# A hybrid decoder layer on one core: the order of the work up to the end of attention, read from a table

## The chip, the core and the metric

The kernel runs on one core of a Trainium2 chip. A core has five engines that run side by side: TensorE (PE, matrix products into PSUM), VectorE (DVE), ScalarE (ACT), GpSimd (POOL) and SyncE (SP), which here issues the transfers between memory and SBUF. Each engine has an instruction stream of its own and carries it out in order; streams meet at semaphores. The metric is the device time of one execution in microseconds, the median of several runs.

## What is computed

One layer (DEPTH is 1) over 1024 tokens of width 1024, in float32:

```python
h = rms_norm(x, norm1_g[layer])
proj = h @ w_in[layer]
q, k, v, glu_a, glu_b = jnp.split(proj, splits, axis=-1)      # 512 columns each
q = rms_norm(q.reshape(bsz, seq, ATTN_HEADS, HEAD_DIM), q_norm_g[layer])
k = rms_norm(k.reshape(bsz, seq, ATTN_HEADS, HEAD_DIM), k_norm_g[layer])
attn = stick_breaking_attention(q, k, v).reshape(bsz, seq, ATTN_WIDTH)
c = glu_a * jax.nn.sigmoid(glu_b)
c = causal_depthwise_conv(c, conv_dw_w[layer], conv_dw_b[layer])      # 31 taps
c = jax.nn.silu(layer_norm(c, conv_ln_g[layer], conv_ln_b[layer]))
x = x + jnp.concatenate([attn, c], axis=-1) @ w_out[layer]
h = rms_norm(x, norm2_g[layer])
gate, val = jnp.split(h @ w_up[layer], 2, axis=-1)
gate = jax.nn.silu(causal_depthwise_conv(gate, ffn_dw_w[layer], ffn_dw_b[layer]))
x = x + (gate * val) @ w_down[layer]
```

Attention has 8 heads of 64 columns, no softmax: the weight of key s for query t is sigmoid(z[t, s]) times the product of (1 - sigmoid(z[t, j])) over the keys j between s and t.

## The kernel before

**Numbers.** A float32 product is made of operands that are each split into a high part and a rest (`hi`, `lo`). Three matmuls (lines 325 to 327, function `mm3`) stand for one product. So each weight and each activation needs a cast (ACT: the high part) and a subtraction (DVE or POOL: the rest).

**Stages.** First part, in one plan of 1874 operations: the norm of x and its transposes (lines 422 to 449), the weights of the projections (loaded at 475, cast at 479, split at 483), the projections of v, of the two halves of the GLU, of q and k (601, 659, 935, 989), the convolution (taps on DVE at 696 to 708, terms on ACT at 722 and POOL at 725, end at 737 to 740, its layer norm at 761 to 820), attention, and the half of the output projection that belongs to the convolution (1345). Second part, in a plan of 237 operations: the half of the output projection that belongs to attention (`opa`), the second norm, and the operands for a Strassen-like form of the up projection. Then the feed-forward part (`up`, and the down projection at 1848) in an order written out by hand.

**Attention.** For each head and each half of the queries: the doubled queries come by a transfer (1124), are transposed (1129), copied with their gain (ACT, 1133) and reduced to the rest (DVE, 1136). For each block of 128 queries the scores `z` are two matmuls (1172, 1173) into one of two PSUM banks; ACT makes 1 - sigmoid of them (1180); DVE runs the product along the keys as a scan (1194); POOL or ACT subtracts one (1199, 1201). Two query blocks go together: per pair of key blocks PE transposes the weights (`wT`, 1221), the high part is copied by ACT or DVE (1230, 1232), the rest made by DVE (1237, 1242), and PE multiplies them with v (`po`, 1249). At the end of a half ACT and DVE copy `po` out (1277, 1280).

**Order.** `Plan.add` (line 94) takes an operation: the engines that it may run on with a cost in ns for each, a function that emits it, a key (about when it is due), the operations that it comes after, and the buffers that it takes (`token`). An operation's number is its place among the calls of `add`. `Plan.run` (line 124) then picks operation after operation: of those that are ready and due (`HORIZON`) it takes the one that can start first by the costs (`PATIENCE` lets an earlier key go first), sends it to the engine where it would end first, hands it its buffers, and calls the function. The order in which functions are called is the order of each engine's stream (`in_order` adds dependences that hold it). The model of `run` adds 60 ns for a hand-over between engines, 130 to POOL, 170 behind PE; it makes POOL and a shared DVE operation (`"DVE2"`) wait for each other; a transfer costs a latency and 2.6 ns per KB.

Of the kernel before, what the change touches and what calls it, by code (L numbers as in the profile page):

```python
# [11 lines left out]
AF = mybir.ActivationFunctionType  # L12
# [28 lines left out]
HORIZON, PATIENCE = 3.0, 150  # L41
# [19 lines left out]


class Plan:


    HAND_OVER, POOL_HAND_OVER = 60, 130
# [5 lines left out]
    class Op:  # L72
        __slots__ = ("cost", "emit", "key", "after", "takes", "end", "engine", "n", "kb", "dmas", "shares")

    def __init__(self, slots, in_turn):
# [20 lines left out]
    def add(self, cost, *args):  # L96
        if not isinstance(cost, dict):
            cost, args = {cost: args[0]}, (lambda eng, f=args[1]: f(),) + args[2:]
        op = Plan.Op()
        op.shares = "DVE2" in cost  # L100
        op.cost, op.emit, op.key = {e.rstrip("2"): c for e, c in cost.items()}, args[0], args[1]
        op.after = list(args[2]) if len(args) > 2 else []
        op.takes = list(args[3]) if len(args) > 3 else []
        op.end, op.engine, op.n, op.kb, op.dmas = None, None, len(self.ops), 512, 1
        self.ops.append(op)
        return op
# [17 lines left out]
    def run(self, busy):  # L124
        at = {e: busy.get(e, 0.0) for e in ("PE", "ACT", "DVE", "POOL", "SP")}
        over = {"PE": 0, "ACT": 100, "DVE": 80, "POOL": 40, "SP": 0}
# [4 lines left out]
        open_ = {op.n: len(set(o.n for o in op.after)) for op in self.ops}  # L131
        nexts = {}
        for op in self.ops:
            for n in set(o.n for o in op.after):
                nexts.setdefault(n, []).append(op)
        ready = [op for op in self.ops if open_[op.n] == 0]
        left = {id(t): len(set(o.n for o in t.users)) for t in self.tokens}
        done, dma, landed, holds = 0, 0.0, [], {"DVE": 0.0, "POOL": 0.0}
        main = sorted(self.ops, key=lambda op: op.key)
        low = 0  # L140
        while done < len(self.ops):
            while main[low].end is not None:
                low += 1
            horizon = main[low].key + HORIZON
            best = None
            for op in ready:
                if op.key > horizon:
                    continue
                slots = self.slots_for(op.takes)
                if slots is None:  # L150
                    continue
                room = max([at_ for at_, _ in slots], default=0.0)
                mine = None
                for e, cost in op.cost.items():
                    r = room
                    for o in op.after:
                        r = max(r, o.end + (0 if o.engine == e else Plan.POOL_HAND_OVER if e == "POOL" else Plan.HAND_OVER)
                                + (170 if o.engine == "PE" and e != "PE" else 0))
                    start = max(r, at[e])
                    if e == "SP":  # L160
                        start = max(start, landed[-8]) if len(landed) > 7 else start
                    if e == "POOL" or e == "DVE" and op.shares:
                        cost += min(cost, max(0, holds["DVE" if e == "POOL" else "POOL"] - start))
                    if mine is None or start + cost < mine[0]:
                        mine = (start + cost, e, cost, start)
                _, e, cost, start = mine
                rank = (max(start - PATIENCE, at[e]), op.key) if op.key <= main[low].key + 1 else (start, op.key)
                if best is None or rank < best[0]:
                    best = (rank, op, e, cost, start)
            assert best is not None, "the plan is stuck"  # L170
            _, op, e, cost, start = best
            for t, slot in zip(op.takes, self.slots_for(op.takes)):
# [5 lines left out]
            if e == "POOL" or e == "DVE" and op.shares:  # L178

                other = "DVE" if e == "POOL" else "POOL"  # L180
                at[other] += min(op.cost[e], max(0, holds[other] - start))
                holds[e] = op.end
            if e == "SP":

                at[e] = start
                for _ in range(op.dmas):
                    at[e] = max(at[e] + 60, landed[-8] if len(landed) > 7 else 0)
                    dma = max(dma, at[e] + (2300 if start < 3000 else 1300)) + op.kb * 2.6 / op.dmas
                    landed.append(dma + 600)
                op.end = landed[-1]  # L190
            else:
                at[e] = op.end - over[e]
            op.emit(e)
            ready.remove(op)
            done += 1
# [4 lines left out]
            for o in nexts.get(op.n, []):  # L200
                open_[o.n] -= 1
                if open_[o.n] == 0:
                    ready.append(o)
# [4 lines left out]
def kernel(  # L208
# [169 lines left out]
    for n in range(2):  # L378
# [12 lines left out]
                in_turn=("nb", "wt", "th", "tl", "thd", "tld", "kst", "vst", "q", "qd"))  # L391
    add = plan.add

    def T(us):

        return (us - FIRST_STAGE) / 8.0
# [28 lines left out]
    def norm_in(t, x, at_):  # L425
# [9 lines left out]
        c = add("DVE", 1290, lambda: nc.vector.scalar_tensor_tensor(xt, xt, d["rs"], g1, op0=ALU.mult, op1=ALU.mult), T(at_), [b])  # L435
# [29 lines left out]
    def weights(name, srcs, shape, at_, key=None, homes=None):  # L465
# [15 lines left out]
        x = add("SP", 3500, load, T(at_ - LEAD_LOAD) if key is None else key, [], [room])  # L481
        a = add("ACT", 1060, high, T(at_ - LEAD_W), [x], d["rooms"])
        b = add({"DVE": 1300, "POOL": 2450}, lambda eng: (nc.vector if eng == "DVE" else nc.gpsimd).tensor_tensor(
# [10 lines left out]
    def differences(blk, key, after, tokens):  # L494
# [17 lines left out]
        x.kb, x.dmas = 1024, 6  # L512
        subs = []
        for n in range(2):
# [4 lines left out]
            subs.append(add({"POOL": 2560}, sub, key, [x]))  # L519
# [13 lines left out]
    def normalized(name, d, o, m, to, at_):  # L533
# [17 lines left out]
        a = add("ACT", 3500, square, T(at_), [c], [r])  # L551
        b = add("POOL", 2700, lambda: rstd(d["rs"], d["sq"], 1.0 / DH), T(at_), [a])
        a = add("ACT", 1850, scale, T(at_), [b])
# [3 lines left out]
    def summed(name, d, o, m, to, at_):  # L557
# [22 lines left out]
        a = add("ACT", 620, square, key, [m], [room, r])  # L580
        b = add("DVE", 690, lambda: nc.vector.tensor_reduce(d["sq"], groups(d["squares"]), axis=AX.X, op=ALU.add), key, [a])
        c = add("POOL", 1900, lambda: rstd(d["rs"], d["sq"], 1.0 / DH), key, [b])
        e = add({"ACT": 1850, "DVE2": 1900}, scale, key, [c])
# [5 lines left out]
    def project(name, parts, ws, t, at_, room):  # L589
# [3 lines left out]
        for k in range(ND):  # L593
# [7 lines left out]
            m = add("PE", 685, products, T(at_ + 0.7 * k), [ws[k // 2]["ready"], h_ready[t][k // 4]] + ([m] if m else [] if name == "v" else list(norm_done)), [] if m else [o])  # L601
# [36 lines left out]
    def glu(c, ws, ats, conv_at, conv_to):  # L638
# [8 lines left out]
        for n, at_ in zip(range(2), ats):  # L647
            gate = None
            for j, part in enumerate("ba"):
                o, m = plan.token("o"), None  # L650
                e = {}
                for k in range(ND):
# [6 lines left out]
                    m = add("PE", 685, products, T(at_ + 5.5 * j + 0.68 * k), [ws[part]["ready"]] + [h_ready[t][k // 4] for t in range(4 * n, 4 * n + 4)] + ([m] if m else []),  # L659
# [27 lines left out]
        last = add({"POOL": 1360, "DVE": 700}, both_sums, key(0, 1), bodies + norm_done + params_ready, [xsum, cacc])  # L687
# [24 lines left out]
        for m in range(HALF + 1):  # L712
            coef = (lambda m=m: tap_sum(c, HALF - 1 - m)) if m < HALF else (lambda: tap(c, 0))
            if m == 0:
                last = add("ACT", 720, lambda coef=coef: nc.scalar.activation(
# [9 lines left out]
            last = add("POOL", 1310, lambda e=e: nc.gpsimd.tensor_tensor(d["c"], d["c"], e["t"], op=ALU.add), key(m, 16), [x, last])  # L725
# [11 lines left out]
        first = add("ACT", 820, shifted, key(1, 1), [b] + co_free, [co_tokens[c]] if c < 3 else [])  # L737
        e1 = add("DVE", 760, lambda: nc.vector.tensor_tensor(d["c"], d["c"], d["a"], op=ALU.subtract), key(1, 1), [last, a, b])
        e2 = add("DVE", 760, lambda: nc.vector.tensor_tensor(out_view()[:, 0, :], d["a"], out_view()[:, 0, :], op=ALU.add), key(1, 1), [first, b, e1])
        e3 = add("DVE", 760, lambda: nc.vector.tensor_tensor(out_view()[:, 1, :], d["c"], d["b"], op=ALU.subtract), key(1, 1), [e1, e2])  # L740
# [11 lines left out]
    def conv_norm(n, at_):  # L752
        half = slice(n * HS, (n + 1) * HS)
        d, normed = {}, []
        for t in range(4):
# [18 lines left out]
            b = add("DVE", 800, stats, k, [a], [r])  # L774
            c = add("POOL", 1450, lambda t=t: rstd(d["rs", t], d["mv", t][:, 1:2], 1.0), k, [b])
            f = add("DVE", 690, normal, k, [c] + conv_normed)
# [4 lines left out]
        for c in range(4):  # L781
# [31 lines left out]
            b = add("ACT", 620, gate, k, [a], [r])  # L813
            f = add("ACT", 620, lambda c=c, dst=dst: nc.scalar.activation(dst(), d["pt", c], AF.Identity, scale=par("lg", c), bias=par("lb", c)), k, [b])
            m = add("POOL", 1310, lambda c=c, dst=dst: nc.gpsimd.tensor_tensor(dst(), dst(), d["gate", c], op=ALU.mult), k, [f])
# [3 lines left out]
            h = add("ACT", 560, high, k, [m] + stores, two if c % 2 == 0 else [])  # L819
            e = add({"DVE": 690, "POOL": 1310}, lambda eng, parts=parts, dst=dst: (nc.vector if eng == "DVE" else nc.gpsimd).tensor_tensor(  # L820
# [7 lines left out]
            if c % 2:  # L828
# [4 lines left out]
                x = add("SP", 4000, store, k, [e])  # L833
                conv_stored[n].append(x)
# [7 lines left out]
    def params():  # L842
# [15 lines left out]
        x.kb = 60  # L858
# [1030 lines left out]
```

## Time and profile before

| | us |
|---|---|
| median of 3 runs | 1120.7 (1119.34 to 1120.95) |
| span of the profiled execution, first to last instruction | 1118.1 |
| PE busy in the span | 1094.5 (98%) |
| DVE busy | 884.7 (79%) |
| ACT busy | 618.6 (55%) |
| POOL busy | 546.6 (49%) |

The span is one execution, taken by the hardware profiler; the runs are timed apart from it. In the lines of the profile, `L1172` is line 1172 of the kernel, `z<-keys` says what an instruction writes and reads, PEld is the loading of a matmul's stationary operand, and an arrow at the end names the instruction that ended the wait in front. The first part of the kernel ends near 430 us, the second near 500 us, and the rest is the feed-forward part.

### The profile page before, as it was taken

What the parts mean: (1) busy time and instruction counts of PE and PEld (TensorE: products, weight loads), DVE (VectorE), ACT (ScalarE), POOL (GpSimd) and SP (SyncE); (2) the same over time, 40 slices, a digit from 0 to 9 for tenths busy, and PEclk for the clock granted to TensorE, in tenths of its full rate; (3) what the DMA queues carried; (4) which work ended last, traced back from release to release, by engine and by line L of the source; (5) the groups of instructions that cost most, each with busy time, mean ns of one, the idle gap of its engine ahead of it and who ended that gap; (6) DMA issues with size and microseconds to landing.
All of it is one profiled execution on the core that took longest, in us unless ns stands there. A gap on an engine that the chain in (4) does not pass through costs nothing.

```text
span 1118.1 us, 14908 instructions
## 1 busy us (share of the span) xinstructions
PE 1094.5 (98%) x5255; PEld 906.2 (81%) x5255; DVE 884.7 (79%) x1188; ACT 618.6 (55%) x1137; POOL 546.6 (49%) x485
## 2 busy tenths in 40 slices
PE   8999999989999999989999999999999999999998
PEld 5888888768888887868888888888888888888887
DVE  6498899579998886889886777777777668787895
ACT  7344567787887674654443433333333378776760
POOL 3165587566344432656332233223323189887770
PEclk9999999999999999999999999999999999999999
DMA  8110500333933224442232231312222482303304
GB/s 286 57 39 8 143 20 24 95 128 88 282 121 113 58 76 151 154 147 76 94 93 96 73 97 59 107 62 97 73 95 76 141 323 83 143 14 146 151 2 150
DMA packets 110234, 118.54 MB, mean 106 GB/s; under 512 B 21105, under 2 KB 89936, under 8 KB 110158
## 3 DMA queue, kind: packets, MB, share of 16 engines
q1 hardware_dynamic: 110014, 117.05, 32.1%
q8 instruction: 42, 0.69, 0.3%
q10 hardware_dynamic: 144, 0.52, 0.1%
q14 instruction: 34, 0.28, 0.1%
HBM read 82.95 MB, written 28.31 MB: 100 GB/s over the span
## 4 chain that ended last, share of the span: by engine, by line
PE 77%; DVE 9%; POOL 4%; ACT 4%; DMA 2%; issue 2%; SPq 0%; POOLq 0%; DVEq 0%; ACTq 0%
PE dn L1848 19%; PE u_S L326 7%; PE u_S L327 7%; PE u_S L325 7%; PE u L327 5%; PE u L326 5%; PE u L325 5%; POOL attn L725 3%; PE po L1249 2%; PE wT L1221 2%; DVE nb L1194 2%; PE opa L325 1%; PE opa L327 1%; PE opa L326 1%; PE z L1172 1%
## 5 line engine op out<-in xcount | busy, mean ns | idle before, releaser
L1848 PE MATMUL dn<-wd,wd 128*128 128x512 f32 x768 | 181.5, 389 | 0.0
L1848 PEld LDWEIGHTS dn<-wd,wd 128*128 128x128 f32 x768 | 144.0, 188 | 30.1 <-DVE c L1851 0.2
L326 PE MATMUL u_S<-bT,aS 128*128 128x512 f32 x264 | 102.8, 389 | 0.8 <-DVE bT L1523 0.8
L327 PE MATMUL u_S<-bT,aS 128*128 128x512 f32 x264 | 102.7, 389 | 0.0
L325 PE MATMUL u_S<-bT,aS 128*128 128x512 f32 x264 | 102.5, 390 | 0.0
L1851 DVE TENSOR_TENSOR c<-dn,c 128x512 f32<-128x512 f32 x120 | 81.0, 684 | 23.9 <-PE dn L1848 23.7
L321 ACT CAST aS<-rawu 128x512 fp32r<-128x512 f32 x63 | 38.9, 621 | 96.2 <-PE u_S L327 66.9
L1753 ACT CAST wd<-rawd 128x512 fp32r<-128x512 f32 x128 | 72.6, 618 | 32.7 <-DMA rawd<-in_w_down_dram 10.8
L1194 DVE TENSOR_TENSOR_SCAN nb<-nb,one 128x128 f32<-128x128 f32 (+4 forms) x64 | 84.8, 1340 | 2.9 <-ACT nb L1180 2.7
L1595 POOL TENSOR_TENSOR s<-rawu 128x512 f32<-128x512 f32 x21 | 29.7, 1415 | 101.7 <-DMA rawu<-in_w_up_dram 92.5
L1752 ACT COPY whole<-rawd 128x512 f32<-128x512 f32 x110 | 63.4, 585 | 24.3 <-DVE wd L1754 11.2
L1754 DVE TENSOR_TENSOR wd<-whole,wd 128x512 fp32r<-128x512 f32 x90 | 59.9, 683 | 16.5 <-ACT wd L1753 9.4
L1601 POOL TENSOR_TENSOR rawu<-rawu 128x512 f32<-128x512 f32 x21 | 29.0, 1381 | 81.2 <-DVE a L322 81.2
L1697 DVE SCALAR_TENSOR_TENSOR y<-gv,cols_a,y 128x1023 f32<-128x1023 f32 (+1 forms) x44 | 59.6, 1355 | 10.2 <-ACT y L1695 10.2
L321 ACT CAST a<-rawu 128x512 fp32r<-128x512 f32 x63 | 39.0, 621 | 49.9 <-PE u_S L327 31.1
L325 PE MATMUL u<-b,a 128*128 128x512 f32 x168 | 65.5, 390 | 0.0
L327 PE MATMUL u<-b,a 128*128 128x512 f32 x168 | 65.5, 390 | 0.0
L326 PE MATMUL u<-b,a 128*128 128x512 f32 x168 | 65.4, 389 | 0.0
L326 PEld LDWEIGHTS u_S<-bT,aS 128*128 128x128 f32 x264 | 49.6, 188 | 11.4 <-POOL raws L1560 1.2
L325 PEld LDWEIGHTS u_S<-bT,aS 128*128 128x128 f32 x264 | 49.5, 188 | 10.7 <-ACT bT L1522 0.4
L327 PEld LDWEIGHTS u_S<-bT,aS 128*128 128x128 f32 x264 | 49.6, 188 | 10.3
L322 DVE TENSOR_TENSOR a<-rawu,a 128x512 fp32r<-128x512 f32 x63 | 47.0, 748 | 13.2 <-ACT a L321 13.2
(343 smaller groups left out, 3213.6 us busy)
## 6 DMA issues: line engine op xcount, KB each, us to landing
rawu<-in_w_up_dram SPq DMA_DIRECT2D x44, 512.0 KB
act_d<-y SPq DMA_DIRECT2D x22, 512.0 KB
rawd<-act_d SPq DMA_DIRECT2D x22, 512.0 KB
rawd<-in_w_down_dram SPq DMA_DIRECT2D x22, 512.0 KB
raw_qk<-in_w_in_dram SPq DMA_DIRECT2D x16, 256.0 KB
rawo<-in_w_out_dram SPq DMA_DIRECT2D x8, 512.0 KB
m<-conv_d SPq DMA_DIRECT2D x16, 256.0 KB
xt<-in_x_dram SPq DMA_DIRECT2D x8, 512.0 KB
```

The lines of the kernel that those rows point to most:

```text
L321: nc.scalar.copy(hi, src)
L322: lo_engine.tensor_tensor(lo, src, f32(hi), op=ALU.subtract)
L325: nc.tensor.matmul(ps, a_hi, b_hi, start=first, stop=False)
L326: nc.tensor.matmul(ps, a_hi, b_lo, start=False, stop=False)
L327: nc.tensor.matmul(ps, a_lo, b_hi, start=False, stop=last)
L1194: nc.vector.tensor_tensor_scan(rev, rev, ones_of[0][:, :w], 0.0, op0=ALU.mult, op1=ALU.max)
L1697: nc.vector.scalar_tensor_tensor(y[:, j:], g[:, :S - j], par("fw", (KF - 1 - j) * NF + f), y[:, j:], op0=ALU.mult, op1=ALU.add)
L1752: nc.scalar.copy(whole, src)
L1753: nc.scalar.copy(t[:, 0], src)
L1754: lo_engine.tensor_tensor(t[:, 1], whole, f32(t[:, 0]), op=ALU.subtract)
L1848: nc.tensor.matmul(ps, a[:, tok], b, start=first and m == 0, stop=last and m == 2, skip_group_check=True)
L1851: nc.vector.tensor_tensor(sums[c][s], ps, sums[c][s], op=ALU.add)
```

## The change

`Plan.run` no longer chooses. It is given a list of operation numbers, `ORDERS[0]` for the first part and `ORDERS[1]` for the second, and goes through it. It still chooses the engine of an operation that may run on several, by the costs, and hands out the buffers. `HORIZON` and `PATIENCE` go. The model by which the engine is chosen is changed: hand-overs by engine, a time for PE's drain and restart, DVE and POOL waiting for each other by the times at which their work overlaps, and transfers by kind (issue, latency, time) in place of a size. Many costs are changed, some DVE operations are marked as shared (`DVE2`), and two operations get a dependence more.

```diff
-HORIZON, PATIENCE = 3.0, 150
+ORDERS = [[int(n) for n in numbers.split()] for numbers in ("""
+0 32 13 1 4 33 41 2 15 14 42 34 35 36 3 38 5 59 7 23 60 37 104 10 43 39 24 105 16 6 44 50 47 40 106 61 45 107 51 48 8
...
+1858 1712 1859 1716 1698 1691 1831 1713 1695 1699 1714 1720 1715 1863 1724 1717 1721 1718 1722 1868 1725 1726 1864
+1860 1719 1861 1869 1723 1727 1728 1870 1729
+""", """
+0 4 3 25 6 5 56 26 7 28 8 27 29 10 1 2 9 30 57 11 59 58 12 13 60 14 32 31 15 17 78 16 79 33 81 80 18 19 34 82 61 21
...
+""")]
...
-    HAND_OVER, POOL_HAND_OVER = 60, 130
+    HAND_OVER = {"ACT": 36, "DVE": 36, "POOL": 86, "PE": 56, "SP": 30}
+    OVER = {"PE": 0, "ACT": 104, "DVE": 82, "POOL": 36, "SP": 0}
+    PE_DRAIN, PE_RESTART, OVERLAP = 163, 100, 150
+    ROWS, PIECE, COLUMNS, MIXED, TWICE, FEW = (360, 1500, 1300), (430, 2000, 770), (390, 2050, 1650), (460, 2200, 870), (630, 1950, 450), (450, 1900, 50)
...
-    def run(self, busy):
+    def run(self, order):
...
+        for op in (self.ops[n] for n in order):
+            slots = self.slots_for(op.takes)
+            assert slots is not None and all(o.end is not None for o in op.after), f"the order is stuck at {op.n}"
+            room = max([at_ for at_, _ in slots], default=0.0)
+            mine = None
+            for e, cost in op.cost.items():
+                r = room
+                for o in op.after:
+                    r = max(r, o.end + (0 if o.engine == e == "PE" else Plan.HAND_OVER[e] + (Plan.PE_DRAIN if o.engine == "PE" else 0)))
+                start = max(r, at[e])
+                if e == "PE" and start > at[e] + 30:
+                    cost += Plan.PE_RESTART
+                if e == "SP":
+                    start = max(start, landed[-8]) if len(landed) > 7 else start
+                if e == "POOL" or e == "DVE" and op.shares:
+                    cost += max([0] + [till - start - Plan.OVERLAP for since, till in holds["DVE" if e == "POOL" else "POOL"] if since <= start])
+                if mine is None or start + cost < mine[0]:
+                    mine = (start + cost, e, cost, start)
+            _, e, cost, start = mine
...
-        b = add({"DVE": 1300, "POOL": 2450}, lambda eng: (nc.vector if eng == "DVE" else nc.gpsimd).tensor_tensor(
+        b = add({"DVE2": 1215, "POOL": 2450}, lambda eng: (nc.vector if eng == "DVE" else nc.gpsimd).tensor_tensor(
...
-        k2 = split_op("k", staged, 0, base - (2.6 if h else EARLY), ready, khl)
+        k2 = split_op("k", staged, 0, base - (2.6 if h else EARLY), ready + (second_used if h else []), khl)
...
-                last = add("PE", 480, products, k, [c] + v2 + ([last] if last else []))
+                last = add("PE", 480, products, k, [c] + v2 + ([last] if last else [prev_last] if g % 2 else []))
...
-    plan.run({})
+    plan.run(ORDERS[0])
...
-    plan.run({})
+    plan.run(ORDERS[1])
```

The rest of the diff is of the kind of the third of these pieces: a cost, a mark `DVE2`, or the kinds of transfers of an operation.

More of the change, by code (lines that the diff above doesn't have):

```diff
@@ L72, with __init__ @@
     class Op:
-        __slots__ = ("cost", "emit", "key", "after", "takes", "end", "engine", "n", "kb", "dmas", "shares")
-    def __init__(self, slots, in_turn):
+        __slots__ = ("cost", "emit", "key", "after", "takes", "end", "engine", "n", "moves", "shares")
+    def __init__(self, slots, in_turn, dma=0.0):
+        self.dma = dma
         self.in_turn, self.given, self.taken = in_turn, {}, {}
@@ L103, in add @@
         op.takes = list(args[3]) if len(args) > 3 else []
-        op.end, op.engine, op.n, op.kb, op.dmas = None, None, len(self.ops), 512, 1
+        op.end, op.engine, op.n, op.moves = None, None, len(self.ops), [Plan.ROWS]
         self.ops.append(op)
@@ L122, in slots_for @@
         return found
-    def run(self, busy):
-        at = {e: busy.get(e, 0.0) for e in ("PE", "ACT", "DVE", "POOL", "SP")}
-        over = {"PE": 0, "ACT": 100, "DVE": 80, "POOL": 40, "SP": 0}
+    def run(self, order):
+        at = {e: 0.0 for e in ("PE", "ACT", "DVE", "POOL", "SP")}
         users = {}
@@ L140, in run @@
[L140 to L172, printed above, removed]
@@ new lines, in run @@
+        left = {id(t): len(set(o.n for o in t.users)) for t in self.tokens}
+        dma, landed, holds = self.dma, [self.dma], {"DVE": [], "POOL": []}
+        assert sorted(order) == list(range(len(self.ops)))
+        for op in (self.ops[n] for n in order):
[17 more added lines that the diff above has]
+            _, e, cost, start = mine
+            for t, slot in zip(op.takes, slots):
@@ L180, in run @@
                 other = "DVE" if e == "POOL" else "POOL"
-                at[other] += min(op.cost[e], max(0, holds[other] - start))
-                holds[e] = op.end
+                holds[e] = (holds[e] + [(start, op.end)])[-4:]
+                if holds[other] and start < holds[other][-1][0] < op.end:
+                    at[other] += max(0, op.end - holds[other][-1][0] - Plan.OVERLAP)
             if e == "SP":
                 at[e] = start
[L186 to L189, printed above, removed]
+                for issue, latency, took in op.moves:
+                    at[e] = max(at[e], landed[-8] if len(landed) > 7 else 0)
+                    dma = max(dma, at[e] + latency) + took
+                    at[e] += issue
+                    landed.append(dma)
                 op.end = landed[-1]
             else:
-                at[e] = op.end - over[e]
+                at[e] = op.end - Plan.OVER[e]
             op.emit(e)
-            ready.remove(op)
-            done += 1
             for t in users.get(op.n, []):
@@ L657, in products @@
                         mm3(e["ps"], hi[:, k, :], lo[:, k, :], h_hi[n][:, k, :], h_lo[n][:, k, :], k == 0, k == ND - 1)
-                    m = add("PE", 685, products, T(at_ + 5.5 * j + 0.68 * k), [ws[part]["ready"]] + [h_ready[t][k // 4] for t in range(4 * n, 4 * n + 4)] + ([m] if m else []),
+                    m = add("PE", 681, products, T(at_ + 5.5 * j + 0.68 * k), [ws[part]["ready"]] + [h_ready[t][k // 4] for t in range(4 * n, 4 * n + 4)] + ([m] if m else []),
                             [] if m else [o])
@@ L685, in key @@
             return T(conv_at + (conv_to - conv_at) * i / of)
-        last = add({"POOL": 1360, "DVE": 700}, both_sums, key(0, 1), bodies + norm_done + params_ready, [xsum, cacc])
+        last = add({"POOL": 1360, "DVE2": 700}, both_sums, key(0, 1), bodies + norm_done + params_ready, [xsum, cacc])
         summed = last
@@ L818, in conv_norm @@
             turned.append(a)
-            h = add("ACT", 560, high, k, [m] + stores, two if c % 2 == 0 else [])
-            e = add({"DVE": 690, "POOL": 1310}, lambda eng, parts=parts, dst=dst: (nc.vector if eng == "DVE" else nc.gpsimd).tensor_tensor(
+            h = add("ACT", 615, high, k, [m] + stores, two if c % 2 == 0 else [])
+            e = add({"DVE2": 690, "POOL": 1310}, lambda eng, parts=parts, dst=dst: (nc.vector if eng == "DVE" else nc.gpsimd).tensor_tensor(
                 parts()[1], dst(), f32(parts()[0]), op=ALU.subtract), k, [h])
@@ L1203 @@
                 a = add("DVE", 130 + 2.1 * w, scan, i - AHEAD_SCAN + 0.3 * u, ones)
-                b = add({"POOL": 100 + 1.03 * w, "ACT": 160 + 0.86 * w}, less, i - AHEAD_SCAN + 0.3 * u, [a])
+                b = add({"POOL": 192 + 0.84 * w, "ACT": 296 + 0.84 * w}, less, i - AHEAD_SCAN + 0.3 * u, [a])
                 ws.append((b, d, nbt, o))
```

85 lines of the change are left out of this document (39 added, 46 removed), and 76 rows, old and new, of the table ORDERS.

## The prediction

> **What bounds the kernel now.** I read the page's head and its chain first, to see which engine carries the end.
>
> ```profile
> span 1118.1 us, 14908 instructions
> PE 77%; DVE 9%; POOL 4%; ACT 4%; DMA 2%; issue 2%; SPq 0%; POOLq 0%; DVEq 0%; ACTq 0%
> ```
>
> TensorE (PE) is 77% of the chain, so only time in which PE stands still can be won; the change adds no matmul and takes none away. The busy times of six stretches (window, length, PE, PEld, DVE, ACT, POOL, PE clock, DMA share, GB/s) say where it stands still.
>
> ```profile
> 0.00:28.00 28.00, 22.58 (x98) 15.33 (x99) 18.05 (x24) 19.81 (x33) 9.24 (x20) 0.94 0.85 286
> 28.00:196.00 168.00, 167.94 (x751) 138.50 (x750) 142.15 (x192) 88.77 (x179) 98.34 (x86) 1.00 0.17 48
> 196.00:252.00 56.00, 51.53 (x272) 40.49 (x270) 35.24 (x57) 42.80 (x114) 33.62 (x45) 1.00 0.36 113
> 252.00:336.00 84.00, 81.24 (x536) 72.02 (x537) 81.77 (x103) 68.01 (x132) 38.67 (x41) 1.00 0.55 162
> 336.00:432.00 96.00, 92.56 (x588) 79.67 (x587) 82.25 (x99) 68.76 (x132) 36.19 (x38) 1.00 0.28 88
> 504.00:896.00 392.00, 392.00 (x1731) 324.64 (x1730) 294.43 (x356) 148.09 (x212) 127.90 (x88) 1.00 0.28 90
> ```
>
> From 28 to 196 us (projections, convolution) PE is full: 167.94 of 168. From 504 us on it is full again, in code that the change leaves alone. The changed part ends near 430 us, so what it can win lies in attention, 196 to 432 us, and in the first 28 us. PE's idle time understates the loss in attention, because the modelled end of a matmul reaches past the start of the next one. The waits of the weight loads (PEld), which go in front of each matmul, have less of that cover; in 196 to 432 us they are (who waited, for whom: us, times, longest):
>
> ```profile
> PEld z L1172 <- ACT nb L1180: 7.3, 13, 1.3
> PEld po L1249 <- DVE tl L1242: 3.1, 6, 1.1
> PEld wT L1221 <- DVE tl L1242: 2.0, 2, 1.3
> PEld op L325 <- DVE attn L1280: 1.7, 2, 0.9
> PEld qk L326 <- DVE lo_qk L483: 1.0, 1, 1.0
> PEld wT L1221 <- ACT nb L1201: 1.0, 1, 1.0
> PEld wT L1221 <- POOL nb L1199: 0.9, 2, 0.8
> ...
> PEld po L1249 <- DVE diagonal L1237: 0.2, 1, 0.2
> ```
>
> The answer has 20 rows from 7.3 down to 0.2, 22.7 us in all. That is the ceiling of the gain in attention, about 2% of the span. No row is large: they are short waits of PE on ACT and DVE.
>
> One of them in the timeline (start, us, engine, line, operation):
>
> ```profile
> 240.57 0.69 ACT L1133 ACTIVATE keys<-qT,qgain 128x512 fp32r<-128x512 f32 x1 [0.25 <-PE qT L1129]
> 241.16 0.38 ACT L1180 ACTIVATE nb<-z 128x256 f32<-128x256 f32 x1
> 241.29 0.75 DVE L1136 SCALAR_TENSOR_TENSOR rest<-qT,qgain,keys 128x512 fp32r<-128x512 f32 x1 [1.37 <-ACT keys L1133]
> ...
> 241.58 0.45 PE L1172 MATMUL z<-keys 128*128 128x384 f32 x1 [1.05 <-ACT nb L1180]
> ```
>
> PE's order has the scores (z) directly behind the query transposes that feed them, and the copy out of the transposes (0.69) and its low half (0.75) lie between: PE stands for 1.05 us. It is an error of order, not of throughput.
>
> **The change, part by part.** *The order.* An operation's number is its place among the calls of `add`, so the tables can be read against the order that the planner makes now. The second table holds the 237 operations of the second part in exactly the order of today; I cost it at nothing, though the engine of an operation that may go to two can still change there. The first table moves its 1874 operations by a median of 10 places. I laid PE's operations of both orders on an axis of pure PE time, with these steps:
>
> ```profile
> 279.74 0.87 PE wT L1221 x8
> 280.62 0.23 PE qk L325
> 282.68 0.95 PE po L1249 x8
> ```
>
> So a transpose is 0.109 us, a matmul of 512 columns 0.23, one of 256 columns 0.119. Between the transposes of a weight block (wT) and the products (po) that use them stand a PE end of 0.16 (a matmul's 0.389 less the step of 0.23), a copy on ACT and a subtraction on DVE:
>
> ```profile
> L1848 PE MATMUL dn<-wd,wd 128*128 128x512 f32 x768 | 181.5, 389 | 0.0
> ...
> L1232 ACT CAST rest<-wT 128x512 fp32r<-128x512 f32 x43 | 24.3, 591 | 7.2 <-PE wT L1221 4.8 <-PE po L1249 2.0
> ...
> L1242 DVE TENSOR_TENSOR tl<-wT,rest x48: 654/681/693, 251.2 to 427.8; 128x512 fp32r<-128x512 f32 x48
> ```
>
> That is 0.16 + 0.59 + 0.68 = 1.43, some 1.55 with two hand-overs (estimate). Other PE work that lies in that distance is a median of 1.9 us now and 3.2 us in the table; distances under 1.55 us are 15 of 80 now and 4 in the table. The same count for scores (query chain, or the bank of two scores before) and for the transposes: with less than 0.3 us to spare are 14 of 96 scores now and 9 after, 4 of 80 transposes and 2, 28 of 80 products and 8.
>
> The terms, with the waits above:
> - products: the rows with po (three, 3.1 to 0.2) sum to 3.7 us; 20 of 28 tight ones go: 2.6 (bounds 0 and 3.7).
> - transposes: the rows with wT sum to 4.5 us, half of the tight ones go: 2.2 (0 and 4.5).
> - scores: the two rows with z sum to 7.6 us. By the count 5 of 14 go, 2.7. But of the twelve places at which scores wait now, eleven have more room in the table, 7.0. The middle: 4.9.
> - banks of conv products and projections (op, qk; three rows, 1.7 to 0.6): 3.0 us; the bank's release depends on ACT's and DVE's load, which the order only shifts. Half: 1.5.
> - the remaining 3.9 us (single waits): a third, 1.3.
>
> Sum 12.5 us.
>
> *DVE as the next in line.* In 252 to 336 us DVE is busy 81.77 of 84 us, so PE can gain there only as DVE gets less or earlier work. Casts that may go to either engine sit on DVE now:
>
> ```profile
> L1230 DVE CAST diagonal<-wT 128x384 fp32r<-128x384 f32 x7 | 3.8, 546 | 0.1
> L1232 DVE CAST rest<-wT 128x512 fp32r<-128x512 f32 x5 | 3.4, 687 | 0.6 <-PE po L1249 0.4
> ```
>
> 7.2 us over attention could move to ACT, which has 16 us free in that stretch. Work that only DVE does does not shrink. I take 1 us off the sum for new waits on DVE (bounds 0 and 9, the latter as if nothing of the stretches after 252 us could be won).
>
> *Keeping two-operand DVE work and POOL apart.* The collisions are in the trace (duration ns min/median/max):
>
> ```profile
> L483 DVE TENSOR_TENSOR lo_glu_b<-raw_glu_b,hi_glu_b x4: 1218/2080/3093, 25.8 to 117.8; 128x1024 fp32r<-128x1024 f32 x4
> L820 DVE TENSOR_TENSOR conv_lo<-conv_out,conv_hi x8: 673/693/1727, 216.5 to 249.4; 128x512 fp32r<-128x512 f32 x8
> ```
>
> The weight splits lose up to 1.9 us each, but before 196 us, beside a full PE: worth nothing. In attention one conv_lo loses 1.0 us, and PE waits for none of them; the 48 subtractions that read wT from PSUM never stretch. So this aim of the change is worth 0 to 1 us; I take 0. [...]
>
> *Transfers.* The queue of SP is in order, and its order changes much. Weight loads of the convolution go later (one stood 41 us of PE work ahead of its first use, now 9), which still covers a landing, a cast and a split (3.46 + 1.07 + 1.22 = 5.8, rows below and above); beside a full PE that costs nothing unless a split collides (3.1 for 1.2 us: 7.7, still covered). At the end, the load of the last x row (operation 1848) moves from 354 to 386 us of 392 on the PE axis, the load of one row of w_out (1868) to 391, behind the stores of four rows (1831 just ahead); behind them in the queue stand the second part's gain row and x rows.
>
> ```profile
> 133.05 1.07 ACT hi_qk L479
> 410.00 3.46 DMA rawo<-in_w_out_dram
> 424.64 1.27 POOL L1353 TENSOR_TENSOR xt<-prod,xt 128x512 f32<-128x512 f32 x1 [5.87 <-ACT prod L1350]
> 429.70 2.35 SPq L1456 DMA_DIRECT2D x<-x_part  x3
> ```
>
> These 5.8 us run from issue to use; with the issue 1 to 6 us ahead of the end, part of it shows at the hand-over, unless the first three rows' products (9 matmuls of 0.23, 2.1 us) and earlier issue in the queue hide it. I take nothing (bounds 0 and 4.5) and keep the rest as a rival. Two new dependences (k split behind the last projections, products behind the previous ones) name work that PE has in front anyway: 0.
>
> *First 28 us.* Loads are reordered (second x row ahead of the weights). PE idles 5.42 us there, mostly behind the first row's norm, which stays first: +0.5 us gained (bounds -1.5 and 2).
>
> Net: 12.5 - 1 + 0.5 = 12 us. The profiled execution would go from 1118.1 to about 1106.1; the median of the runs lies 2.6 us above the span (1120.7), so 1108.7.
>
> **Rivals.**
> - *Nearly all waits close.* The table doubles the room before products, so 18 to 20 us of 22.7 could go: 1101.5. For it: eleven of twelve waiting scores get room. Against it: DVE is full for 84 us. The next instruction does start before the last one's recorded end, by 0.08 us in these rows, but the stretch's 81.77 us counts an overlap once, so DVE has no hidden room in it.
>
> ```profile
> 242.07 0.69 DVE L820 TENSOR_TENSOR conv_lo<-conv_out,conv_hi 128x512 fp32r<-128x512 f32 x1
> 242.68 0.68 DVE L1194 TENSOR_TENSOR_SCAN nb<-nb,one 128x256 f32<-128x256 f32 x1
> ```
>
> [...]
> - *DVE is the bound.* Waits move from one PE operation to the next, and only the 196 to 252 us stretch (4.5 us of PE idle) improves: gain 3 to 6, 1116. For it: 97% busy.
> - *Slower: the hand-over through SP's queue.* The store of the last row waits for two POOL sums, they for the load 1848, and the second part's x rows queue behind. That chain is 3.46 + 2 x 1.27 + the store; if it starts only when the last slot comes free, the second part starts 6 us late, and each further wait in the queue (POOL waits of up to 5.87 for prod) adds to it. It decides from 12 us of delay; with 15, 1123.7.
> - *The order hardly reaches the engines*, since waits are set by banks: within 0.2%, 1120.
>
> **How the numbers follow.** Forecast (gain 8 to 16) 0.60; nearly all closes 0.14; DVE bound 0.14; hardly any effect 0.06; slower 0.06. A measurement of this kernel tells about 0.2% (2.2 us) from no change. Faster: 0.60 + 0.14 + 0.13 of the DVE case = 0.87; same 0.07; slower 0.06. The range leaves out the two worst cases (0.12) and gains over 20 us: 1100.5 to 1117.5.
>
> **What would show it.** Right: the PEld waits of 196 to 432 us fall from 22.7 to about 10, the rows z and po most; SP's issue of the x rows (429.70 now) comes near 418; DVE stays over 90% from 252 us on; 504 us on is only shifted. Wrong: waits of PE on DVE that grow; the first opa matmuls waiting for loo or x; L483 waits of PE before 196 us.

## The result and the profile after

| | before | after |
|---|---|---|
| median of the runs, us | 1120.3 (4 runs, 1119.34 to 1120.95) | 1114.1 (4 runs, 1113.49 to 1115.17) |
| span of the profiled execution, us | 1118.1 | 1112.4 |

The ratio is 0.9947, 95% interval [0.9933, 0.9961]: 6.2 us less, where 12 were forecast (5.7 by the spans of the two profiled executions). Time and sign lie in the forecast's range, the gain is half of it. It lies under the 8 to 16 us of the forecast itself and beside the 3 to 6 of the rival "DVE is the bound", whose mechanism did not come, as the windows below show.

To see where the other half went, PE's instructions of both traces were laid on one axis of their own pure time (0.227 us for 512 columns, 0.109 for a transpose, and so on). The time of the trace beyond that axis is what PE stood still or ran slowly:

| stretch of the work | before | after | difference |
|---|---|---|---|
| to 28 us | 7.6 | 7.6 | 0 |
| 28 to 196 us | 2.1 | 3.4 | +1.3 |
| 196 us to the last `po` (429.4 before, 419.9 after) | 20.7 | 9.9 | -10.8 |
| the hand-over, some 15 us from there | 0.1 | 1.5 | +1.4 |
| rest of the second part, to the S products | 5.6 | 8.0 | +2.4 |
| feed-forward (the pure step is set a little too long) | -0.7 | -0.7 | 0 |

So attention won 10.8 us, near the forecast, and 5.1 us were given back in three places that the forecast put at nothing.

The windows of after, same columns as in the prediction:

```profile
28.00:196.00 168.00, 167.11 (x750) 137.27 (x749) 140.44 (x192) 89.22 (x184) 96.33 (x84) 1.00 0.15 44
196.00:252.00 56.00, 53.80 (x296) 44.38 (x295) 41.51 (x63) 47.77 (x132) 38.63 (x50) 1.00 0.42 134
252.00:336.00 84.00, 83.37 (x540) 73.01 (x540) 80.38 (x99) 62.28 (x130) 46.93 (x54) 1.00 0.49 145
...
504.00:896.00 392.00, 392.00 (x1731) 324.61 (x1730) 292.28 (x358) 150.52 (x217) 126.60 (x89) 1.00 0.29 95
```

From 252 to 336 us PE goes from 81.24 to 83.37 of 84 us. DVE has about the same work (81.77, now 80.38) and no longer holds PE up there. ACT's work falls by 5.7 us there and POOL's grows by 8.3. What moved shows in the groups by line between 196 and 432 us, first before, then after. It is the subtraction of one from a block of attention:

```profile
L1201 ACT ACTIVATE nb<-nb,minus_one 128x1024 f32<-128x1024 f32 (+7 forms) x31 | 25.6, 824 | 9.1 <-DVE nb L1194 9.0
...
L1199 POOL TENSOR_SCALAR nb<-nb 128x512 f32<-128x512 f32 (+7 forms) x33 | 22.3, 674 | 47.2 <-DVE nb L1194 42.7 <-ACT keys L1099 2.5 <-ACT rest L1232 1.9
```

```profile
L1265 POOL TENSOR_SCALAR nb<-nb 128x896 f32<-128x896 f32 (+7 forms) x52 | 37.6, 724 | 57.3 <-DVE nb L1260 44.7 <-PE wT L1287 6.5 <-ACT rest L1298 2.4
...
L1267 ACT ACTIVATE nb<-nb,minus_one 128x640 f32<-128x640 f32 (+5 forms) x12 | 8.1, 684 | 0.5 <-DVE nb L1260 0.2
```

31 of them stood on ACT, now 12 do. Though the diff leaves the choice of the engine to the planner, with its new order, costs and times the planner chooses another engine for 70 of the 238 operations of the first part that have a choice, and for 7 of 51 of the second.

The waits of the weight loads in the same stretch of after:

```profile
PEld z L1238 <- ACT nb L1246: 3.2, 10, 0.6
PEld kT L1160 <- issue: 1.6, 3, 0.9
PEld qk L389 <- DVE lo_qk L547: 1.3, 2, 1.1
PEld opa L388 <- ACT m L1528: 1.0, 1, 1.0
PEld po L1315 <- DVE tl L1308: 0.9, 2, 0.5
PEld op L388 <- DVE attn L1346: 0.8, 3, 0.3
PEld opa L389 <- DVE loo L1463: 0.6, 1, 0.6
```

The 20 rows sum to 12.8 us; without the two rows of `opa`, which belong to the next part, 11.2 of 22.7 are left. Scores, products and transposes won, and the three rows of banks that the prediction counted fell from 3.0 to 1.2 us; but other waits came (`kT` 1.6, more of `qk`), and all rows of `qk` and `op` together only go from 4.0 to 3.4.

**The three losses.** First, at 110 us (timeline of after, all engines): two weight splits behind each other on DVE, each against an addition on POOL, then PE, which waits for the second.

```profile
107.12 1.80 DVE L547 TENSOR_TENSOR lo_glu_a<-raw_glu_a,hi_glu_a 128x1024 fp32r<-128x1024 f32 x1
...
107.91 1.96 POOL L789 TENSOR_TENSOR attn<-attn,attn_first 128x512 f32<-128x512 f32 x1
...
108.84 2.11 DVE L547 TENSOR_TENSOR lo_glu_b<-raw_glu_b,hi_glu_b 128x1024 fp32r<-128x1024 f32 x1
...
110.09 2.02 POOL L789 TENSOR_TENSOR attn<-attn 128x512 f32<-128x512 f32 x1
...
111.01 0.50 PE L390 MATMUL glu_b<-h_hi,lo_glu_b 128*128 128x512 f32 x1 [0.69 <-DVE lo_glu_b L547]
```

Alone such a split takes 1.22 us, the first addition 1.09, the second 1.30. Up to 430 us, the DVE instructions that took over 0.1 us more than the usual of their line and shape were 7 before (6.7 us too long) and are 10 after (8.9 us); over the whole trace they were 57 (42.8 us) and are 59 (43.4). The change did not keep the two engines apart.

Second, the hand-over at 420 us, DVE's timeline of after and the two PE rows:

```profile
419.42 1.22 DVE L1463 TENSOR_TENSOR loo<-rawo,hio 128x1024 fp32r<-128x1024 f32 x1
420.93 1.23 DVE L1463 TENSOR_TENSOR loo<-rawo,hio 128x1024 fp32r<-128x1024 f32 x1 [0.29 <-ACT attn L1343]
...
425.99 1.29 DVE L1551 TENSOR_TENSOR x<-opa,x 128x512 f32<-128x512 f32 x2 [0.77 <-DMA x<-x_part]
```

```profile
420.69 0.50 PE L389 MATMUL opa<-loo,m 128*128 128x512 f32 x1 [0.27 <-DVE loo L1463]
...
426.82 0.47 PE L388 MATMUL opa<-hio,m 128*128 128x512 f32 x1 [0.62 <-DVE x L1551]
```

The first product waits for the split of its row of w_out, the third for a bank that the sum with x frees, and that sum for the transfer of x. Before, PE had neither wait.

Third, the first products of the feed-forward part, with their waits before and after:

```profile
481.12 0.63 PE L1510 MATMUL h2T<-ident_r,h 128*128 128x128 f32 x4 [1.13 <-DVE h L1502]
482.71 0.50 PE L325 MATMUL u<-b,a_first 128*128 128x512 f32 x1 [0.96 <-ACT b L1522]
483.52 0.47 PE L326 MATMUL u<-b,a_first 128*128 128x512 f32 x1 [0.31 <-DVE b L1523]
483.83 0.40 PE L327 MATMUL u<-b,a_first 128*128 128x512 f32 x1
```

```profile
473.38 0.63 PE L1577 MATMUL h2T<-ident_r,h 128*128 128x128 f32 x4 [1.11 <-DVE h L1569]
475.12 0.50 PE L388 MATMUL u<-b,a_first 128*128 128x512 f32 x1 [1.11 <-ACT b L1589]
475.94 0.77 PE L389 MATMUL u<-b,a_first 128*128 128x512 f32 x1 [0.32 <-DVE b L1590]
476.50 0.63 PE L390 MATMUL u<-b,a_first 128*128 128x512 f32 x1
476.93 0.63 PE L388 MATMUL u<-b,a_first 128*128 128x512 f32 x1
```

The waits are alike (2.40 and 2.54 us in sum), but after them matmuls follow each other at 0.43 us instead of 0.227. The windows of the two traces name the cause, the granted clock (before, then after):

```profile
477.00:487.00 10.00, 7.60 (x36) 5.78 (x35) 7.51 (x13) 7.00 (x14) 4.93 (x6) 1.00 0.66 206
```

```profile
477.00:478.00 1.00, 1.00 (x4) 0.81 (x3) 0.95 (x2) 1.00 (x4) 0.00 (x0) 0.50 0.00 0
```

### The profile page after: what moved, and what is told of

The parts are those of the page before. It is cut to its first block, busy times and chain, and to the rows that moved or that the text cites. A ratio compares the mean times of both kernels' runs of the same rounds, so it can differ in the third digit from the quotient of the medians.

```text
span 1112.4 us, 14919 instructions
## 1 busy us (share of the span) xinstructions
PE 1092.3 (98%) x5255; PEld 907.1 (82%) x5255; DVE 885.6 (80%) x1181; ACT 608.7 (55%) x1139; POOL 565.6 (51%) x509
## 4 chain that ended last, share of the span: by engine, by line
PE 86%; POOL 5%; DVE 3%; ACT 2%; issue 2%; DMA 1%; SPq 0%; POOLq 0%; DVEq 0%; ACTq 0%
PE dn L1916 19%; PE u_S L388 7%; PE u_S L390 7%; PE u_S L389 7%; PE u L390 5%; PE u L389 5%; PE u L388 5%; PE po L1315 3%; POOL attn L789 3%; PE wT L1287 3%; PE z L1238 2%; PE z L1239 1%; PE op L388 1%; PE op L389 1%; PE op L390 1%
## 5 line engine op out<-in xcount | busy, mean ns | idle before, releaser
L1919 DVE TENSOR_TENSOR c<-dn,c 128x512 f32<-128x512 f32 x120 | 81.7, 687 | 27.4 <-PE dn L1916 26.7
L1260 DVE TENSOR_TENSOR_SCAN nb<-nb,one 128x896 f32<-128x896 f32 (+7 forms) x64 | 85.1, 1342 | 1.6 <-ACT nb L1246 1.3
L1822 DVE TENSOR_TENSOR wd<-whole,wd 128x512 fp32r<-128x512 f32 x90 | 60.1, 686 | 12.5 <-ACT wd L1821 6.2
L789 POOL TENSOR_TENSOR attn<-attn,attn_first 128x512 f32<-128x512 f32 x42 | 48.5, 1156 | 40.8 <-ACT attn L779 32.4
L1265 POOL TENSOR_SCALAR nb<-nb 128x896 f32<-128x896 f32 (+7 forms) x52 | 37.6, 724 | 57.3 <-DVE nb L1260 44.7
L390 PEld LDWEIGHTS u_S<-bT,aS 128*128 128x128 f32 x264 | 49.6, 188 | 10.3
L389 PEld LDWEIGHTS u_S<-bT,aS 128*128 128x128 f32 x264 | 49.5, 188 | 10.3
```

What stands on the lines that cost most here:

```text
L389: nc.tensor.matmul(ps, a_hi, b_lo, start=False, stop=False)
L390: nc.tensor.matmul(ps, a_lo, b_hi, start=False, stop=last)
L789: last = add("POOL", 1092, lambda e=e: nc.gpsimd.tensor_tensor(d["c"], d["c"], e["t"], op=ALU.add), key(m, 16), [x, last])
L1260: nc.vector.tensor_tensor_scan(rev, rev, ones_of[0][:, :w], 0.0, op0=ALU.mult, op1=ALU.max)
L1822: lo_engine.tensor_tensor(t[:, 1], whole, f32(t[:, 0]), op=ALU.subtract)
L1919: nc.vector.tensor_tensor(sums[c][s], ps, sums[c][s], op=ALU.add)
```

## The experiments

Three questions: does attention's gain come from the order or from the other engines; what are the losses worth; can they be had back. For the engines, `Plan.run` got a dictionary of operations whose engine is given. An operation that is not in it still goes where the costs send it:

```diff
-    def run(self, order):
+    def run(self, order, engines={}):
...
             for e, cost in op.cost.items():
+                if engines.get(op.n, e) != e:
+                    continue
```

Medians in us; the kernel before ran beside each group, at 1119.0 to 1119.3.

| run | median | ratio to before, interval |
|---|---|---|
| the change again (e5) | 1113.2 | 0.9956 [0.9943, 0.9969] |
| new order, 70 on old engines, 26 more moved (e1) | 1139.9 | 1.0185 [1.0171, 1.0198] |
| old order, new engines (e2) | 1132.9 | 1.0123 [1.0109, 1.0137] |
| 31 subtractions on old engines (e8) | 1122.4 | 1.0026 [1.0014, 1.0039] |
| 16 casts on old engines (e9) | 1119.2 | 1.0001 [0.9991, 1.0010] |
| 23 others on old engines (e10) | 1123.4 | 1.0035 [1.0022, 1.0048] |
| second part: 7 on old engines, 5 more moved (e3) | 1112.3 | 0.9937 [0.9925, 0.9950] |
| four matmuls more (e4) | 1111.6 | 0.9931 [0.9919, 0.9944] |
| hand-over eased (e6) | 1113.0 | 0.9949 [0.9936, 0.9961] |
| cast behind (e7) | 1110.9 | 0.9934 [0.9922, 0.9947] |
| together (e11) | 1109.6 | 0.9911 [0.9897, 0.9926] |
| and two exchanges (e12) | 1108.7 | 0.9904 [0.9888, 0.9921] |

**Order or engines.** The table of the change, with the 70 operations of the first part on their old engines:

```diff
+ENGINES = [{70 operations of the first part: engine of before}, {}]
-    plan.run(ORDERS[0])
+    plan.run(ORDERS[0], ENGINES[0])
```

> The order table of the change, but in the first part each of the 70 operations whose engine differs goes to the engine that it had before. Theory (the order makes the gain): PE still gains about 11 us between 196 us and the last po, and the time stays near the changed kernel's 1114.1, 1113 to 1115.5. Rival (the gain comes from the other engine choices, above all the subtractions of one that moved from ACT to POOL and the casts): the gain in attention falls to under 5 us and the time is 1117 to 1120.

And the order of before with the engines of after:

```diff
 ORDERS = [[int(n) for n in numbers.split()] for numbers in ("""
-0 32 13 1 4 33 41 2 15 14 42 34 35 36 3 38 5 59 7 23 60 37 104 10 43 39 24 105 16 6 44 50 47 40 106 61 45 107 51 48 8
+{the 1874 operations as the old planner put them}
...
+ENGINES = [{all operations with a choice: engine of after}, {the same}]
```

> The order of before, with the engine of each operation as in the changed kernel (and its two added dependences). Theory (order): no gain in attention, 1119 to 1122. Rival (engines): 1114 to 1117.

The first of these two runs is not what its text says. Its dictionary names the 70 operations alone, and the planner, free in the other 168 choices, sent 26 of them elsewhere than before or the change, 14 of these from ACT to DVE. The trace shows it: of the 80 casts of weight blocks DVE makes 20 there, 12 before and 8 in the change. So it takes 26.7 us more than the change and 20.9 more than before with a third set of engines, and it doesn't decide between its theory and its rival. It does show that the order alone fixes little: PE's order is exactly that of the change, and yet the last `po` comes 25 us later, 20 of them lost in attention.

The second run gives all choices, and its engines are exactly those of the change. Both its theory and its rival fell: 13.9 us more than before. The new engines without the new order are worth nothing. (The planner also hands out buffers by its modelled times, and 90 operations had other buffers than before there; what that costs was not separated.)

For the order without the new engines, the 70 operations in three groups, each put back alone, with the engines of all others given as in the change:

```diff
+ENGINES = [{31 subtractions of one, line 1270}, {}]
+ENGINES = [{16 casts of weight blocks, line 1323}, {}]
+ENGINES = [{23 others}, {}]
```

> The changed kernel, with the 31 subtractions of one in attention that changed engine on their old one (25 back from POOL to ACT, 6 from ACT to POOL), all else as changed. The first run of this study, with all 70 old engines, took 26.7 us more than the changed kernel. Theory (ACT carries out its stream in order; a subtraction that the table places for POOL stands on ACT in front of casts and waits there for its scan): this group is the largest share, 8 to 15 us more than the changed kernel, 1121 to 1128, lost between 250 and 440 us. Rival (only the whole set of engines matters, each group alone little): under 3 us more.

> The changed kernel, with the 16 casts of weight blocks that changed engine on their old one (10 from ACT to DVE, 6 from DVE to ACT). Theory: DVE is full there, so four casts more on it and their places cost 2 to 5 us: 1115 to 1118. Rival: under 2 us.

> The changed kernel, with the other 23 operations that changed engine on their old one (copies and scales of v, k, q, weight splits, a few in the convolution). Theory: the 6 us that the run with all old engines lost at 76 us (the GLU product waiting 4.5 us for the bank of v) come from three scales of k and their copies, and with some 3 us more in the convolution and the key chains this gives 1120 to 1124. Rival: under 3 us more.

They cost 9.2, 6.0 and 10.2 us. The first and the third cost what their theories said, the casts more than expected, and the rival, that only the whole set matters, fell in all three runs. Each group alone takes the whole gain away. (Their sum, 25.4, is not to be compared with the 26.7 of e1, where other operations moved too. Buffers are the same in the run on the casts, and but for five in the one on the subtractions; in the third run 133 operations had others.) The mechanism is seen best in the third group, where PE waited 4.3 us at 76 us. DVE's and PE's timeline of that run, then ACT's of the change at the same place:

```profile
73.89 6.30 DVE L776 SCALAR_TENSOR_TENSOR conv_b<-cpad,cols_b,conv_b 128x512 f32<-128x512 f32 x8
80.10 0.75 DVE L596 COPY v<-v 128x256 f32<-128x256 f32 x2
```

```profile
80.99 0.77 PE L392 MATMUL glu_a<-h_hi,hi_glu_a 128*128 128x512 f32 x1 [4.34 <-DVE v L596]
```

```profile
76.89 0.62 ACT L592 COPY v<-v 128x256 f32<-128x256 f32 x2
```

The copy out of the bank that PE needs stands in DVE's stream behind eight taps of the convolution. In the table its place was made for ACT, where it runs at once. The wait cost more than itself: the matmuls behind it take 0.77, 0.63 and 0.63 us where the three ahead of it took 0.39, as in the change at a granted clock of 0.50, and 13 of them follow each other at 0.43 us instead of 0.227, another 2.7 us. In that execution, the slowest of the five, with a clock of 0.993 (0.996 in the profiled one of the change), the two are 7 us.

In the first group it is the subtraction of one; ACT's, POOL's and PE's rows of that run:

```profile
280.64 0.60 ACT L1067 ACTIVATE squares<-qk 128x512 f32<-128x512 f32 x1 [1.79 <-PE qk L394]
281.30 0.48 ACT L1300 CAST diagonal<-wT 128x384 fp32r<-128x384 f32 x1
281.68 1.15 ACT L1271 ACTIVATE nb<-nb,minus_one 128x1024 f32<-128x1024 f32 x1
...
282.07 0.20 POOL L383 TENSOR_SCALAR rs_qk<-sq_qk 128x8 f32<-128x8 f32 x1 [5.12 <-DVE sq_qk L1076]
...
282.88 0.98 PE L1291 MATMUL wT<-ident_r,nb 128*128 128x128 f32 x7 [1.36 <-ACT nb L1271]
```

Its scan had ended at 279.6 and POOL stood idle for 5 us, but on ACT it came behind squares of `qk`, for which ACT itself stood idle for 1.79 us, and behind a cast, and PE waited 1.36 us. In the change a subtraction of that size runs on POOL at 279.2 us.

**The losses.** The 7 operations of the second part on their old engines (the planner moved 5 of the other 44 as well), and four matmuls in the pause:

```diff
+ENGINES = [{}, {7 operations of the second part: engine of before}]
```

```diff
         (ah, al), (bh, bl) = A[a], B[b]
+        if f == 0 and a == "11":
+            for _ in range(4):
+                nc.tensor.matmul(ps, ah[:, 0, :], ah, start=True, stop=True)
```

> The changed kernel, but the 7 operations of the second part whose engine changed go to their old engine. The second part gave 3.8 us back. If the engine choices are the cause, the time falls by 2 to 3.8 us to 1110.5 to 1112; my theory gives them only the longer wait of u for a (1.5 against 0.8 us at the first S products): 1113.3 to 1114.

> Four matmuls more that stand in front of the first product of the feed-forward part, in its bank, with operands that are ready long before; they fill about 0.9 us of the 1.1 us in which PE waits for b at 474 us. Theory (the granted clock falls since PE stood still for 2.5 of 3.6 us, and 7 matmuls then take 0.43 instead of 0.23 us): the slow matmuls go, 1.5 us less, 1112.4 to 1113. Rival (the clock falls for another reason): no change, 1113.8 to 1114.8.

With these engines the wait of `u` for `a` (1.5 us) is gone and one of 0.5 us for `bT` takes its place, 1.2 us less in the trace; more matmuls were slow in that execution (a clock of 0.90 from 470 to 504 us, 0.95 in the change) and took it back there. The median is 0.9 us under the change's, and the intervals overlap: the sign is likely, not shown, and what the 7 alone are worth is open. In the run with four matmuls more the trace shows what the clock theory said:

```profile
470.00:480.00 10.00, 8.17 (x38) 6.13 (x38) 7.22 (x12) 6.29 (x12) 5.80 (x6) 1.00 0.45 133
```

The clock stays at 1.00 (0.83 in the same window of the change), the 1.7 us are gone in the trace, and the median is 1.6 us lower. Over the whole execution the clock was 0.998 to 1.000 in its five runs and 0.996 to 0.998 in the nine of the change.

> The changed kernel once more, beside the next two runs and on their chip. By the first measurement 0.9947 of before. It also shows whether its two losses are there in each execution: slow matmuls after 474 us (1.5 us lost) and the hand-over (1.5 us).

It showed both: the clock falls again (0.95 from 470 to 504 us, as in the first trace), though its three pauses are only 1.91 us in sum (PE's idle time from 470 to 476 us), and the hand-over loses 1.5 us again. Beyond 28 us the two traces differ by at most 0.2 us up to attention's end.

> The changed kernel with the hand-over to the second part eased by the tables alone: the row of w_out that the first product needs is loaded and split first of the four (its split stood at 419.4 us, and the first product waited for it), and the gain row is loaded behind the first three x rows. Theory (the hand-over gives back what these two waits cost, 0.44 and 0.79 us of the 1.5): 0.6 to 1.2 us less than the changed kernel. Rival (the products after them would wait for the same transfers anyway): no difference.

```diff
-1871 1829 1565 1601 1865
+1862 1829 1565 1601 1865
...
-0 4 3 25 6 5 56 26 7 28 8 27 29 10 1 2 9 30 57 11 59
+4 3 25 6 5 56 0 26 7 28 8 27 29 10 9 30 57 11 1 2 59
```

(1862 to 1864 and 1871 to 1873, the load, cast and split of two rows of w_out, change places; 0 loads the gain row, 1 and 2 copy it, 3, 25 and 56 load x rows.)

The rival was nearly right: both waits go (0.44 and 0.71 us with PE's restart, in the trace of the change beside it), and a new one of 0.58 us (0.41 of it standing still) comes at 430 us, for the norm `h`, whose gain row now lands behind three x rows. The median does not tell the rest from nothing.

> The changed kernel, but on ACT the cast of a that waits for the landing of rawu (473.5 us) goes behind the two casts of b that stand behind it, and the cast that the first product needs goes ahead of the copy. Before and after have this order alike. Theory (PE waits at 474 us for a cast that is ready to run at 472.3 and stands behind one that isn't): the two waits of 1.1 and 0.3 us shrink, the clock stays up, 2 to 3 us less than the changed kernel. Rival (the products of S stand behind a chain on DVE and POOL that this doesn't shorten): the first 2 us come back as a longer wait at 491 us, under 1 us.

Here 175 and 177 are the transposes, 221 is the cast that waits for rawu, 178 the copy, 180 and 181 make `b`:

```diff
-157 175 221 192 178 153 193 176 180 154 177 181 160
+157 175 192 180 178 153 193 176 154 177 181 221 160
```

Theory and rival each got half. The clock stays up (1.00 from 470 to 504 us) and the median falls by 2.3 us, but the wait for `a` grows from 1.5 to 2.8 us:

```profile
487.79 0.50 PE L394 MATMUL u<-b,a 128*128 128x512 f32 x1 [2.79 <-DVE a L389]
```

**Together.**

> The changed kernel with what helped, by tables alone: the row of w_out that is needed first goes first, the gain row is loaded between the first and the second x row and copied behind the first two sums, the cast that waits for rawu goes behind the casts of b, and the 7 operations of the second part have their old engines. From the changed kernel's 1113.2: 2.3 for the cast, 1.0 for the engines, 0.7 to 1.2 for the hand-over, 1109 to 1110. If the gains exclude each other (each only uncovers the wait for a at 485 us): 1110.5 to 1111.

```diff
-4 3 25 6 5 56 0 26
+4 3 0 25 6 5 56 26
```

(That line against the run on the hand-over; the other edits are those shown.) 1109.6, as the sum said. With the gain row between the first two x rows, PE loses 1.0 us from the last `po` to 450 us, where the change lost 2.4; the wait for `a` is 0.86 us. Here all 51 choices of the second part are given, so that its engines are exactly those of before.

> The run before (all that helped together, 0.9911 of before) and two exchanges more. At 107 us the split of glu_b goes ahead of that of glu_a, which is used 4 us later: both collide with additions on POOL (1.80 and 2.11 us for 1.22), and PE waited 0.7 to 1.1 us for the second. At 472 us DVE makes the norm of the last row's second half ahead of another row's sum: PE waited 1.27 us for it. Theory (each of the two is what PE waits for, and nothing stands right behind it): 0.9 and 0.6 us less, 1108.0 to 1108.5. Rival at 107 us: glu_a then waits as long. Rival at 472 us: the wait for a at 486 us grows by what is won, 1109 to 1109.6.

```diff
-397
+394
...
-394
+397
...
-398
+395
...
-395
+398
...
-175 192 180 178 153 193 176
+175 180 178 153 176 192 193
```

At 107 us the theory holds. The splits collide as before, but the one that is wanted first now ends first (DVE's timeline), and PE's wait is gone, 1.0 us less in the trace:

```profile
106.33 1.80 DVE L551 TENSOR_TENSOR lo_glu_b<-raw_glu_b,hi_glu_b 128x1024 fp32r<-128x1024 f32 x1
108.05 2.11 DVE L551 TENSOR_TENSOR lo_glu_a<-raw_glu_a,hi_glu_a 128x1024 fp32r<-128x1024 f32 x1
```

At 472 us neither was quite right: the norm comes 0.6 us earlier, the wait for `a` goes, and waits of 0.62 us for `b` and 0.73 for `bT` come. 1108.7, the lowest of all: 10.5 us under before, 4.5 under the change. It is 0.8 us under the run before it, and their intervals overlap: that the two exchanges together gain is likely, and shown only for the wait at 107 us.

## Why the prediction was right, and where it wasn't

- **Attention** (12.5 less 1 us): 10.8. By rows: scores 7.6 to 3.2 (4.9 forecast, 4.4 came), products 3.7 to 1.3 (2.6; 2.4), transposes 4.5 to 0.3 (2.2; 4.2), banks of `op` and `qk` 3.0 to 1.2 (1.5; 1.8). The single waits, of which 1.3 us were to go, grew from 3.9 to 5.2, and the transposes, above their forecast, make up for them. DVE held little up, but seems to have little room: the run on the casts, with 16 moved and four more on DVE, some 2.5 us of work, cost 6.0.
- **The reason behind that number failed in part.** I counted the room in PE's order alone and took the engines of the rest nearly as given (casts might move to ACT). The run with the 31 subtractions put back has PE's order of the change, and so the same room on that axis, and loses 8 us more in attention. The count was a fair measure only since the engines chosen fit the table, and that its sum came out near is in part luck. The largest group that moved was the subtraction of one, mostly from ACT to POOL, which no step of the prediction saw.
- **28 to 196 us, "costs nothing unless a split collides"**: the mis-sized term, 1.3 us. I took a single collided split, 3.1 for 1.2 us, as covered. Two collided one behind the other, the second was the one wanted, and PE waited; exchanging them ends that wait, 1.0 us.
- **Keeping DVE and POOL apart, worth 0**: right for attention, with the wrong sign at 110 us. There a weight split on DVE took 2.11 us instead of 1.22, and the additions on POOL beside it 1.96 and 2.02 instead of 1.09 and 1.30. In the trace of before, the 8 of 19 splits on DVE beside which POOL ran nothing took 1.21 to 1.23 us, and each of the five over 1.4 us (1.45 to 3.09) lay beside a two-input operation on POOL of 512 columns or more. Why the two lengthen each other was not shown.
- **The hand-over, "I take nothing (bounds 0 and 4.5)"**: 1.4 us, inside the bounds, and the signs named for it came: products waiting for loo and for x. The queue of SP was not late (x rows at 420.2 instead of 418); the last split in DVE's order and the landing of x, for which the sum at 425.99 us waited 0.77 us, were.
- **The second table, "at nothing"**: 2.4 us, the largest miss. Some 1.7 is the clock (0.50 for 3.4 us in the trace) and 0.7 the wait for `a`, which is gone in the run with other engines there (e3): the engine choice that the prediction named and did not price. What the clock does to the medians is smaller: over the whole execution it was 0.995 to 1.000 in the runs of before and 0.996 to 0.998 in those of the change, so before too is likely to lose some of it in some executions, though not in the profiled one.
- **The first 28 us** (+0.5): nothing came, inside its bounds.

Open: the new order with exactly the old engines was not run. Why the old order with the new engines loses 6 us more than before near 196 us and 5 more in the rest of attention was not taken apart. How often the clock falls in executions of before is not seen in a trace.

## What to carry to other kernels

An order table is made for a set of engines. Where a planner still chooses the engine by costs, read which operations change engine before reading the order, and if a table is kept, keep the engines in it: putting 16 casts back cost as much as the change had won. An experiment on engines gives all of them: where only those that had changed were given, the planner moved others. A stretch in which PE is full has no cover to give away when two late things stand in one queue, and a pause of PE can cost again behind it: 2.5 us of pauses and then 1.7, 4.3 us and then 2.7.

## What the runs showed of the hardware

In the change the granted clock fell to 0.50 though PE never stood still for longer than 1.11 us at once there, and it was down for some 3.4 us: 0.88 from 475 to 476 us, 0.50 from 476 to 479, 0.92 from 479 to 480, 1.00 behind that. It fell behind these three pauses, at 474 us in the change, in six of the profiled executions: from 468 to 500 us the clock is 0.95 in both of the change, in e6, e8 and e9, and 0.89 in e3. In e1, e2 and e10 it fell behind the later wait for `a`, a single pause of some 2.7 us (0.80 from 511 to 518 us, 0.81 from 505 to 512 and 0.80 from 496 to 502), and in these three elsewhere too (from 196 to 252 us it is 0.97 in e1 and 0.95 in e2; in e10 the matmuls behind the wait of 4.34 us are slow). The length of the pauses alone doesn't tell these executions apart: 1.91 us in sum were enough in e5, 2.40 in the same place of before were not (1.00 from 477 to 487 us), nor was a single pause of 2.79 us in e7 (1.00 from 484 to 494).

What decides whether the clock falls was not shown. It differs between executions of one kernel: over the whole execution it was 0.995, 0.996, 0.999, 0.999 and 1.000 in the five of e3, so a kernel can keep or lose part of the clock from one execution to the next.
